# Strassen groups whose outer pairs alternate product by product, and the end of an attention head on VectorE alone

## The chip, the cores and the metric

The kernel runs on one core of one Trainium2 chip. The metric is the device time of one execution in microseconds (us); a kernel is timed several times and its median is taken. The engines are TensorE (PE, matrix products; PEld is its loading of weights), VectorE (DVE), ScalarE (ACT), GpSimd (POOL) and SyncE (SP), whose queue issues the transfers.

## What is computed

One step of a layer with two branches on the same normalised input, for 2048 frames of a new stream and 64 frames of a running one (2112 rows, 17 blocks of 128 of which the last, "the sample", has 64 rows). Everything is fp32.

```
xn = rms_norm(x, norm_gain);  u = xn @ w_in
xa, za, q, k, v, zb, ga, gb = split_in(u)
h, h_last = rglru(conv(xa), ...);      ya = h * silu(za)
q = rms_norm(q per head half);         k = rms_norm(k per head half)
o = diff_attn(q, k, v, ...)            # softmax minus lam * softmax
yb = rms_norm(o) * subln_gain * ... * silu(zb)
m = sigmoid(ga) * (ya @ w_proj_a) + sigmoid(gb) * (yb @ w_proj_b)
y = x + m @ w_out
```

## The kernel before

**Products.** An fp32 product is made of three matmuls on halves: each operand is cut into a high part (ScalarE's cast) and a low part (a subtraction), and high by high, high by low and low by high are added up in PSUM (lines 63, 64 and 65).

**Stages.** The Hawk branch (to about 492 us), stage a (six projections of 1024 columns: v, q/k of heads 0 to 3, zb, q/k of heads 4 to 7, ga, gb, to about 1625 us), the attention (eight heads, to about 2596 us), and stage d (out_a, out_b, out_y). Stages a and d are objects of the class `Stage`, which runs *groups*; a group is one 2112x1024 by 1024x1024 product.

**A Strassen group.** The 16 whole blocks of x form eight *pairs* (block i and block i+8). The weight is cut in four quarters, a pair into four too, and a Strassen-Winograd scheme makes seven products of 12 matmuls instead of eight for each pair, 56 products a group. Seven weights are needed: B11, B21, B22 and T1 to T4. The sample block takes five short slots without Strassen, at the end of the group. A *slot* is one product on TensorE; `tick()` closes it, `at(slot, task)` places the work of the other engines in a slot, and the four engines run in this written order (`manual_schedule`); only SP's queue is ordered by a scheduler.

**Around the products.** `plan_w` says in which slot a weight is loaded, subtracted (`sub`, line 126, VectorE, in two halves) and cut (`cut`: ScalarE line 133, then low halves on VectorE and GpSimd, line 135). `plan_x` does the same for the x of a pair: S1 and S2 on VectorE, S3 and S4 on GpSimd (line 163), high halves on ScalarE (167), low halves on VectorE (S2 and A12) and GpSimd (the other five) (170). `pair` issues the seven products and takes them out of PSUM: five additions on VectorE (217, 223, 228, 238, 243) and two copies on ScalarE (213, 233). What is done with the result depends on the group. In a q/k group the squares are summed (763), the inverse root is made (776, 780, 55 to 57), the two results are scaled (785) and, some slots later, transposed by TensorE (800) and taken out on ScalarE and VectorE (815, 817). In gates it is a sigmoid (735), for zb a product as well (740).

**The end of a head.** The head's result `o` lies in SBUF as 17 blocks. `finish` makes an inverse root `y` per row with Newton steps (1151 to 1155, 55 to 57). For heads 0 to 6 GpSimd multiplies each block by its column of y (1186); then `weigh` loads up to four blocks of the gate, `zt`, and GpSimd multiplies (1166). `part` transposes the block on TensorE (1173), VectorE scales the result into `yt` (1175) and SP stores it to yb_d (1176). For the last head VectorE does both products. `zt` and `yt` have two buffers each. Meanwhile the next head works: its maxima are taken by VectorE straight from PSUM (950, 1062), and its sums of exponentials are combined by GpSimd (975, 976).

## Time and profile before

| | us |
|---|---|
| median of three runs | 3159.47 (3156.75 to 3160.89) |
| the profiled execution's own time | 3151.77 |
| its span | 3150.0 |
| TensorE busy | 2858.8 |
| VectorE / ScalarE / GpSimd busy | 2107.5 / 1624.6 / 1647.2 |
| stage a / attention / stage d, about | 1132 / 970 / 546 |

Busy times of the engines overlap; they don't add up to the span. The span is the part of the execution that the trace covers, 1.8 us less than its time. TensorE's mean granted clock was 0.959 of full speed.

### The profile page before, as it was taken

To read this page: it belongs to the slowest core of one execution; us is meant where nothing else is said; L and a number is where in the kernel's file an instruction comes from. 1 tells how busy PE (TensorE), PEld (TensorE's weight loads), DVE (VectorE), ACT (ScalarE), POOL (GpSimd) and SP (SyncE) were. 2 spreads that over 40 slices of the span, in tenths; PEclk is the share of its full clock that TensorE was granted. 3 is DMA by queue.
4 is the path that set the end of the run, shared out by engine and by line. 5 is a ranking of instruction groups with operands and counts; after the bars stand their busy time and mean duration, and the time that the engine had idled before them with its cause. 6 is when DMAs were issued, how large, how long until landed. Compare 5 with 4: busy or idle time off the path is not lost. (4 is left out here: it accounts for less than half of the span.)

```text
span 3150.0 us, 44022 instructions
## 1 busy us (share of the span) xinstructions
PE 2858.8 (91%) x14808; PEld 2404.1 (76%) x14808; DVE 2107.5 (67%) x4074; ACT 1624.6 (52%) x3111; POOL 1647.2 (52%) x1145
## 2 busy tenths in 40 slices
PE   6999997999979899899989898898898879989898
PEld 6888885778768687687868787787787767868687
DVE  8777777378884888737346675675675774485864
ACT  7677764244453445534337666566576552233421
POOL 0000005475565755657535665565565557797853
PEclk9999998999989999999999999999999999999899
DMA  4121132345543446533366345344343334555453
GB/s 138 63 74 60 67 107 94 119 137 150 178 153 121 132 145 180 163 107 117 110 166 172 105 116 140 102 119 137 98 123 108 107 97 154 184 190 204 158 171 127
DMA packets 356674, 408.99 MB, mean 130 GB/s; under 512 B 48448, under 2 KB 242400, under 8 KB 356448
## 3 DMA queue, kind: packets, MB, share of 16 engines
q1 hardware_dynamic: 356448, 406.18, 41.9%
q8 instruction: 118, 1.93, 0.3%
q14 instruction: 108, 0.88, 0.1%
HBM read 272.22 MB, written 131.37 MB: 128 GB/s over the span
## 5 line engine op out<-in xcount | busy, mean ns | idle before, releaser
L63 PE MATMUL acc<-w,xq 128*128 128x512 f32 x2016 | 810.7, 402 | 31.0 <-DVE s L223 16.4
L64 PE MATMUL acc<-w,xq 128*128 128x512 f32 x2016 | 800.2, 397 | 31.4 <-DVE w L135 29.0
L65 PE MATMUL acc<-w,xq 128*128 128x512 f32 x2016 | 800.4, 397 | 9.6 <-POOL xq L170 9.5
L170 POOL TENSOR_TENSOR xq<-xq 128x512 fp32r<-128x512 f32 x360 | 535.5, 1500 | 377.7 <-ACT xq L167 236.3
L163 POOL TENSOR_TENSOR xq<-xq 128x512 f32<-128x512 f32 x144 | 203.1, 1410 | 551.7 <-DVE xq L163 547.7
L63 PEld LDWEIGHTS acc<-w,xq 128*128 128x128 f32 x2016 | 387.8, 192 | 120.3 <-issue 30.3
L64 PEld LDWEIGHTS acc<-w,xq 128*128 128x128 f32 x2016 | 387.8, 192 | 112.9 <-DVE w L135 31.5
L65 PEld LDWEIGHTS acc<-w,xq 128*128 128x128 f32 x2016 | 387.2, 192 | 95.4 <-POOL xq L170 10.6
L167 ACT CAST xq<-xq 128x512 fp32r<-128x512 f32 x504 | 297.6, 619 | 27.7 <-DVE xq L163 13.7
L1003 PE MATMUL accv<-v,tw 128*128 128x128 f32 x2176 | 302.6, 283 | 8.0 <-ACT o L1015 8.0
L950 DVE TENSOR_SCALAR_CACHE_REDUCE S<-pk,far 128x1024 f32<-128x1024 f32 x224 | 225.7, 1014 | 120.9 <-PE pk L938 112.9
L937 PE MATMUL pk<-k,Q 128*128 128x512 f32 (+2 forms) x640 | 270.8, 424 | 29.5 <-DVE mp L958 17.8
L1003 PEld LDWEIGHTS accv<-v,tw 128*128 128x128 f32 x2176 | 278.0, 198 | 12.7 <-ACT o L1015 10.1
L968 ACT ACTIVATE S<-S,nm 128x1920 f32<-128x1920 f32 (+7 forms) x128 | 208.9, 1632 | 70.3 <-DVE nm L967 68.9
L233 ACT COPY s<-acc 128x512 f32<-128x512 f32 x72 | 42.2, 587 | 391.7 <-PE acc L65 366.4
L996 ACT COPY tw<-ptt 128x512 f32<-128x512 f32 (+1 forms) x288 | 157.4, 556 | 160.2 <-PE ptt L995 158.8
L938 PE MATMUL pk<-k,Q 128*128 128x512 f32 (+2 forms) x640 | 236.6, 376 | 1.6 <-DMA Q<-ql_d 1.5
L64 PE MATMUL accb<-x,wh 128*128 128x384 f32 (+3 forms) x656 | 232.9, 355 | 2.9 <-DVE x L503 2.9
L63 PE MATMUL accb<-x,wh 128*128 128x384 f32 (+3 forms) x656 | 234.4, 357 | 0.2 <-ACT x L502 0.2
L976 POOL TENSOR_TENSOR S<-S,S 128x2048 f32<-128x2048 f32 (+3 forms) x64 | 230.3, 3599 | 4.2
L65 PE MATMUL accb<-x,wl 128*128 128x384 f32 (+3 forms) x656 | 232.4, 354 | 0.0
L975 POOL TENSOR_SCALAR S<-S,cf 128x2048 f32<-128x2048 f32 (+3 forms) x64 | 102.6, 1603 | 238.0 <-DVE cf L974 115.2
(244 smaller groups left out, 5561.8 us busy)
## 6 DMA issues: line engine op xcount, KB each, us to landing
xq<-xn_d SPq DMA_DIRECT2D x192, 256.0 KB, 3.9
w<-in_wg SPq DMA_DIRECT2D x72, 512.0 KB, 5.4
Q<-qh_d SPq DMA_DIRECT2D x128, 128.0 KB, 2.9
Q<-ql_d SPq DMA_DIRECT2D x128, 128.0 KB, 2.9
raw<-in_ckT SPq DMA_DIRECT2D x32, 512.0 KB, 3.7
raw<-in_cv SPq DMA_DIRECT2D x32, 512.0 KB, 3.9
raw<-in_w1b SPq DMA_DIRECT2D x32, 256.0 KB, 3.0
ya_d<-SZ SPq DMA_DIRECT2D x16, 512.0 KB, 3.3
```

The lines of the kernel that those rows point to most:

```text
L63: nc.tensor.matmul(out, shi, mhi, start=start, stop=False, **kw)
L64: nc.tensor.matmul(out, shi, mlo, start=False, stop=False, **kw)
L65: nc.tensor.matmul(out, slo, mhi, start=False, stop=stop, **kw)
L163: eng.tensor_tensor(q[dst], q[x], q[y], op=op)
L167: nc.scalar.copy(xs[nm][0], q[nm])
L170: eng.tensor_tensor(xs[nm][1], q[nm], xs[nm][0].bitcast(F32), op=ALU.subtract)
L937: nc.tensor.matmul(pk[:, o], Q[0][:, m, qs], kk, start=True, stop=False)
L938: nc.tensor.matmul(pk[:, o], Q[1][:, m, qs], kk, start=False, stop=True)
L950: nc.vector.tensor_scalar(s[:, k0 : k0 + f], pk[:, :f], far[:, h : h + 1], None, op0=ALU.add, op1=ALU.max, accum_out=mp[:, cx["j"] : cx["j ...
L968: nc.scalar.activation(s[:, :n], s[:, :n], AF.Exp, bias=nm, accum_out=sc[m])
L976: nc.gpsimd.tensor_tensor(S[0][:, :n], S[0][:, :n], S[1][:, :n], op=ALU.add)
L1003: nc.tensor.matmul(acc[:, r, :], tw[:, j, :], hd[kt // 8][1][:, kt % 8, :], start=kt == r == 0, stop=kt == 2 * p + 1)
```

## The change

Four things are changed.

1. **Order of the pairs.** The items of a group are now `(0, 1)`, `(2,)`, `(3,)`, the sample, `(4,)`, `(5,)`, `(6, 7)`. In `(0, 1)` and `(6, 7)` the two pairs alternate product by product, so a weight serves two products in a row and the next one is wanted two slots later. The order of the products is A11·B11, S1·T1, S2·T2, A12·B21, S3·T3, S4·B22, A22·T4.
2. **Sums in PSUM.** S2·T2, S3·T3 and A22·T4 are added onto the bank of A11·B11 (`bx`), S4·B22 onto that of S1·T1 (`by`). Of a pair VectorE makes three additions (lines 234, 238, 242 after the change) and ScalarE four copies.
3. **Plans.** The weights' subtractions and cuts stand in other slots: counted from the group's start, T1's subtraction -7, B11's cut -6, T2's subtraction -5, T1's cut -4, T2's cut -2, the subtractions of T3 and T4 both -1, the cuts of B21, T3, B22, T4 at 0, 2, 4, 6. VectorE makes three low halves of a pair's x (S2, A12, A22) and the sample's, GpSimd four. q and k are taken out of PSUM in the slot of their transposes. Buffers are rings for each kind.
4. **End of a head.** Scaling by y and product with zt are one VectorE instruction per block (scalar_tensor_tensor, line 1172 after the change) for every head; `zt` has three buffers. GpSimd does neither any more.

The core of the diff:

```
-ITEMS = [0, 1, 2, 3, 4, 5, 6, 7, "s"]
+ITEMS = [(0, 1), (2,), (3,), "s", (4,), (5,), (6, 7)]
...
-        at(b - 16, lambda: (load("B11", 0), load("B12", 1)))
-        at(b - 13, lambda: sub("T1", "B12", "B11"))
-        at(b - 10, lambda: load("B22", 3))
-        at(b - 9, lambda: (load("B21", 2), cut("B11")))
-        at(b - 7, lambda: sub("T2", "B22", "T1"))
-        at(b - 6, lambda: cut("T2"))
-        at(b - 5, lambda: sub("T3", "B22", "B12", "B12"))
-        at(b - 4, lambda: sub("T4", "B21", "T2", "T2"))
-        for i, nm in enumerate(("T3", "T1", "B21", "T4", "B22")):
-            at(b - 3 + i, lambda nm=nm: cut(nm))
+        at(b - 13, lambda: (load("B11", 0), load("B12", 1)))
+        at(b - 8, lambda: load("B22", 3))
+        at(b - 7, lambda: sub("T1", "B12", "B11"))
+        at(b - 6, lambda: cut("B11"))
+        at(b - 5, lambda: sub("T2", "B22", "T1"))
+        at(b - 4, lambda: (load("B21", 2), cut("T1")))
+        at(b - 2, lambda: cut("T2"))
+        at(b - 1, lambda: (sub("T3", "B22", "B12", "B12"), sub("T4", "B21", "T2", "T2")))
+        for i, nm in enumerate(("B21", "T3", "B22", "T4")):
+            at(b + 2 * i, lambda nm=nm: cut(nm))
...
+        off = b - s[0]
+        for nm, k, eng in zip(("A11", "S1", "S2", "A12", "S3", "S4", "A22"), s, (G, G, V, V, G, G, V)):
+            at(k + off - 4, lambda nm=nm: hi(nm))
+            at(k + off - 3, lambda nm=nm, eng=eng: lo(nm, eng))
...
+        bx, p1 = bank(), self.small()
+        prod(bx, "A11", "B11", True)
+        nc.scalar.copy(p1, bx)
+        yield
+        by, p5 = bank(), self.small()
+        prod(by, "S1", "T1", True)
+        nc.scalar.copy(p5, by)
+        yield
         u2 = self.small()
+        prod(bx, "S2", "T2", False)
+        nc.scalar.copy(u2, bx)
+        yield
+        bz = self.pz.tile([P, 512], F32, name="acz")
+        prod(bz, "A12", "B21", True)
+        V.tensor_tensor(p1, p1, bz, op=ALU.add)
+        done(item, 0, p1)
+        yield
+        prod(bx, "S3", "T3", False)
+        V.tensor_tensor(p5, p5, bx, op=ALU.add)
+        done(item + 8, 1, p5)
+        yield
+        prod(by, "S4", "B22", False)
+        V.tensor_tensor(u2, u2, by, op=ALU.add)
+        done(item, 1, u2)
+        yield
+        prod(bx, "A22", "T4", False)
         c21 = self.small()
+        nc.scalar.copy(c21, bx)
         done(item + 8, 0, c21)
...
-                zt = wk.tile([P, 4, P], F32, name="zt")
+                zt = wk.tile([P, 4, P], F32, name="zt", bufs=3)
...
-                eng = nc.gpsimd if h < NH - 1 else nc.vector
-                eng.tensor_tensor(o[:tn, b : b + nb, :], o[:tn, b : b + nb, :], zt[:tn, :nb, :], op=ALU.mult)
-                book("pool" if h < NH - 1 else "dve", pe[0] + 2.0, 0.33 * nb)
+                for j in range(nb):
+                    k = b + j
+                    nc.vector.scalar_tensor_tensor(
+                        o[:tn, k, :], o[:tn, k, :], y[:tn, k - t0 : k - t0 + 1], zt[:tn, j, :],
+                        op0=ALU.mult, op1=ALU.mult,
+                    )
+                book("dve", pe[0] + 2.0, 0.25 * nb)
...
-            for j in range(t0 if h < NH - 1 else whole, t0 + n):
-                tn = TOK[j][1]
-                nc.gpsimd.tensor_scalar(
-                    o[:tn, j, :], o[:tn, j, :], y[:tn, j - t0 : j - t0 + 1], 1.0, op0=ALU.mult, op1=ALU.mult
-                )
-                book("pool", pe[0] + 2.0, 0.35)
```

VectorE at the end of a head, before: the last Newton steps, then the next head's work (cf is a factor of the softmax, SA and SB hold scores, mps their maxima).

```order
L55 SCALAR_TENSOR_TENSOR e_17032<-yo 128x17
L56 TENSOR_TENSOR e_17032<-e_17032,q_15301 128x17
L57 SCALAR_TENSOR_TENSOR yo<-e_17032,yo 128x17
L973 RECIPROCAL cf<-s_16602 128x1
L1062 TENSOR_SCALAR SA,mps<-pk,far 128x1024
L974 SCALAR_TENSOR_TENSOR cf<-cf,s_16601,neglam 128x1
L1062 TENSOR_SCALAR SA,mps<-pk,far 128x1024
L1062 TENSOR_SCALAR SB,mps<-pk,far 128x1024
L1062 TENSOR_SCALAR SB,mps<-pk,far 128x896
L1067 ISA SB,mps<-pk,bands 128x128
L1067 ISA mps 128x1
L1175 TENSOR_SCALAR yt<-ptt,gs 128x512
```

The same place after the change:

```order
L55 SCALAR_TENSOR_TENSOR e_16566<-yo 128x17
L56 TENSOR_TENSOR e_16566<-e_16566,q_14876 128x17
L57 SCALAR_TENSOR_TENSOR yo<-e_16566,yo 128x17
L1172 SCALAR_TENSOR_TENSOR o<-o,yo,zt 128x128 x12
L978 RECIPROCAL cf<-s_16183 128x1
L1067 TENSOR_SCALAR SA,mps<-pk,far 128x1024
L1172 SCALAR_TENSOR_TENSOR o<-o,yo,zt 128x128 x4
L979 SCALAR_TENSOR_TENSOR cf<-cf,s_16182,neglam 128x1
L1172 SCALAR_TENSOR_TENSOR o<-o,yo,zt 64x128
L1067 TENSOR_SCALAR SA,mps<-pk,far 128x1024
L1184 TENSOR_SCALAR yt<-ptt,gs 128x512
L1067 TENSOR_SCALAR SB,mps<-pk,far 128x1024
```

The 17 new instructions stand directly behind the Newton steps, 12 of them ahead of the first maximum of line 1067 (1062 before).

VectorE where the first q/k group passes into zb, before (217 to 243 are additions from PSUM, 763 a sum of squares, 817 an eviction of q, 126 and 135 a weight's subtraction and low half):

```order
L763 TENSOR_REDUCE va<-s_7925 128x8
L817 SCALAR_TENSOR_TENSOR s_8019<-ptx,gq,s_8017 128x512
L243 TENSOR_TENSOR s_7833<-s_7833,acc 128x512
L135 TENSOR_TENSOR w_8047<-w_8001,w_8046 128x1024
L763 TENSOR_REDUCE va<-s_7962 128x8
L776 TENSOR_SCALAR va<-va 128x16
L817 SCALAR_TENSOR_TENSOR s_8067<-ptx,gq,s_8065 128x512
L126 TENSOR_TENSOR w_7693<-w_7898,w_7693 128x1024 x2
L780 RECIPROCAL ya<-sra 128x16
L55 SCALAR_TENSOR_TENSOR tmpa<-ya 128x16
L56 TENSOR_TENSOR tmpa<-tmpa,va 128x16
L57 SCALAR_TENSOR_TENSOR ya<-tmpa,ya 128x16
```

The same passage after the change (775 is the sum of squares, 787, 792 and 55 to 57 the inverse root, 797 the scales, 828 the eviction of q, 135 a weight's subtraction, 145 its low half, 181 the low half of an x):

```order
L797 TENSOR_TENSOR sc<-sc,ya 128x512 x2
L775 TENSOR_REDUCE va<-sf 128x8
L135 TENSOR_TENSOR w_7617<-w_7763,w_7617 128x1024 x2
L135 TENSOR_TENSOR w_7856<-w_7882,w_7856 128x1024 x2
L775 TENSOR_REDUCE va<-sf 128x8
L145 TENSOR_TENSOR w_8008<-w_7882,w_8007 128x1024
L828 SCALAR_TENSOR_TENSOR sf<-ptx,gq,sf 128x512
L775 TENSOR_REDUCE va<-sf 128x8
L787 TENSOR_SCALAR va<-va 128x16
L181 TENSOR_TENSOR x_8013<-xS_7859,x_8013 128x512
L828 SCALAR_TENSOR_TENSOR sf<-ptx,gq,sf 128x512
L792 RECIPROCAL ya<-ya 128x16
```

The subtractions of T3 and T4 stand together now, and the roots and scales of two pairs one behind the other around them; the next root and its scales follow behind these rows.

SP's queue where gb, the last group of stage a, passes into the attention, before (gb_d takes the group's results, 64x512 are the sample's; Q, k and bands are loads of the attention):

```order
L737 DMA gb_d<-s_14150 128x512
L737 DMA gb_d<-s_14058 128x512
L882 DMA k_14307<-kl_d 64x2x1024
L911 DMA Q_14301<-qh_d 64x2x256
L912 DMA Q_14301<-qh_d 64x2x256
L911 DMA Q_14304<-ql_d 64x2x256
L261 DMA s_14213<-s_14211 64x512
L912 DMA Q_14304<-ql_d 64x2x256
L261 DMA s_14225<-s_14223 64x512
L898 DMA band<-strip_d 64x256
L899 DMA band<-strip_d 64x192
L900 DMA band<-neg 64x64
L737 DMA gb_d<-s_14211 64x512
```

The same place after the change:

```order
L749 DMA gb_d<-sc 128x512
L1108 DMA vn<-out_v 64x128
L1046 DMA raw<-in_ckT 128x1024 x3
L749 DMA gb_d<-sc 128x512
L886 DMA k_14259<-kh_d 64x2x1024
L749 DMA gb_d<-sc 128x512 x2
L887 DMA k_14259<-kl_d 64x2x1024
L916 DMA Q_13876<-qh_d 64x2x256
L917 DMA Q_13876<-qh_d 64x2x256
L916 DMA Q_13879<-ql_d 64x2x256
L917 DMA Q_13879<-ql_d 64x2x256
```

The loads of Q stood ahead of the sample's stores to gb_d; now all stores to gb_d stand ahead of them.

## Rows read from the trace of the kernel before

**Rows 1.** The page's busy time and share of the span of each engine.
```profile
PE 2858.8 (91%) x14808; PEld 2404.1 (76%) x14808; DVE 2107.5 (67%) x4074; ACT 1624.6 (52%) x3111; POOL 1647.2 (52%) x1145
```

**Rows 2.** What TensorE waited for, whole span: us in total, times, longest.
```profile
PE ptt L1173 <- DVE yt L1175: 31.5, 5, 7.6
PE ptx L800 <- DVE s L785: 30.7, 14, 7.3
PE acc L64 <- DVE w L135: 29.0, 6, 7.9
PE ptt L1173 <- POOL o L1166: 28.7, 17, 4.2
```

**Rows 3.** Stretches of the v and first q/k group: length, busy us of engines, clock.
```profile
492.30:682.90 190.60, 177.47 (x730) 138.92 (x730) 97.81 (x96) 64.71 (x106) 103.00 (x67) 0.94 0.37 118
682.90:892.50 209.60, 186.18 (x831) 148.44 (x830) 184.94 (x243) 97.11 (x178) 124.77 (x81) 0.95 0.50 152
```

**Rows 4.** A stretch behind a head's last wait, same columns: PEclk is the granted clock.
```profile
1905.90:1912.70 6.80, 4.41 (x17) 4.13 (x18) 4.71 (x25) 2.37 (x6) 0.00 (x0) 0.50 0.45 123
```

**Rows 5.** Timeline of GpSimd at one head's end: start, length, instruction.
```profile
1882.37 5.91 POOL L1186 TENSOR_SCALAR o<-o,yo 128x128 f32<-128x128 f32 x17
...
1889.50 1.65 POOL L975 TENSOR_SCALAR S<-S,cf 128x1664 f32<-128x1664 f32 x1
...
1892.34 3.72 POOL L976 TENSOR_TENSOR S<-S,S 128x1664 f32<-128x1664 f32 x1
1896.03 2.50 POOL L1166 TENSOR_TENSOR o<-o,zt 128x512 f32<-128x512 f32 x2
```

**Rows 6.** Timeline of SP's queue in the same stretch.
```profile
1892.41 5.36 SPq L1162 DMA_DIRECT2D zt<-zb_d  x2
```

**Rows 7.** Timeline of VectorE in the same stretch; brackets hold its idle time.
```profile
1907.39 0.75 DVE L1175 TENSOR_SCALAR yt<-ptt,gs 128x512 f32<-128x512 f32 x1 [13.51 <-DMA yb_d<-yt]
```

**Rows 8.** Line 437 on VectorE: duration in ns, min/median/max, first and last start.
```profile
L437 DVE SCALAR_TENSOR_TENSOR wl<-raw,chan,wh x128: 342/347/360, 9.3 to 425.5; 128x128 fp32r<-128x128 f32 x128
```

**Rows 9.** Chain that ended last, from 3141 us: start, length, what.
```profile
3141.02 0.23 PE acc L254
...
3142.37 2.25 DMA s<-s
```

**Rows 10.** VectorE by line in stage a: busy us and mean ns of one.
```profile
L170 DVE TENSOR_TENSOR xq<-xq 128x512 fp32r<-128x512 f32 x96 | 96.4, 1004 | 0.0
L135 DVE TENSOR_TENSOR w<-w,w 128x1024 fp32r<-128x1024 f32 x40 | 86.2, 2174 | 4.1 <-ACT w L133 4.1
L126 DVE TENSOR_TENSOR w<-w,w 128x1024 f32<-128x1024 f32 x40 | 68.3, 1750 | 0.0
L785 DVE TENSOR_TENSOR s<-s,ya 128x512 f32<-128x512 f32 (+1 forms) x68 | 56.8, 877 | 1.2
L763 DVE TENSOR_REDUCE va<-s 128x8 f32<-128x512 f32 (+1 forms) x68 | 46.0, 677 | 0.0
...
L55 DVE SCALAR_TENSOR_TENSOR tmpa<-ya 128x16 f32<-128x16 f32 (+1 forms) x34 | 22.6, 664 | 1.2
```

**Rows 11.** TensorE's waits from 855 to 905 us, first q/k group to zb.
```profile
PE ptx L800 <- DVE s L785: 14.7, 3, 7.3
```

**Rows 12.** TensorE's waits from 490 to 530 us, start of stage a.
```profile
PE acc L65 <- POOL xq L170: 6.7, 1, 6.7
PE acc L64 <- DVE w L135: 6.2, 1, 6.2
```

**Rows 13.** TensorE's waits from 2590 to 2615 us, start of stage d.
```profile
PE acc L63 <- ACT w L133: 5.5, 1, 5.5
```

**Rows 14.** DMA issues on the page: transfers, KB each, median us to landing.
```profile
Q<-qh_d SPq DMA_DIRECT2D x128, 128.0 KB, 2.9
```

**Rows 15.** VectorE at 863.37 on the timeline, and a table of the stretch around it.
```profile
863.37 4.49 DVE L785 TENSOR_TENSOR s<-s,ya 128x512 f32<-128x512 f32 x2
...
861.50:868.30 6.80, 3.40 (x16) 2.33 (x15) 6.66 (x8) 3.21 (x5) 5.42 (x3) 1.00 0.55 171
```

More of the change, by code (lines that the diff above doesn't have):

```diff
@@ L122, in sub @@
         def sub(dst, x, y, over=None):
[L123 removed]
+            q[dst] = q[over] if over else self.wtile(pick=pick)
             for i in range(2):
@@ L232, in pair, with prod @@
-        c11 = self.small()
-        nc.scalar.copy(c11, b1)
-        done(item, 0, c11)
-        self.tick()
-        self.product(b3, x["A22"], w["T4"], False, True, True)
+        def prod(out, a, b, first):
+            self.product(out, x[a], w[b], first, True, not first)
+            if item == 7:
+                self.wfree.extend(w[b][2])
+        bx, p1 = bank(), self.small()
[3 more added lines that the diff above has]
+        by, p5 = bank(), self.small()
@@ L289, in run @@
             ws = {}
-            self.plan_w(wsrc, ws, b)
-            for it in ITEMS:
-                xs = {}
-                self.plan_x(xsrc, it, xs, b - 5 if it == 0 and b > 0 else b)
-                plan.append((it, xs, ws, out, b))
-                b += 5 if it == "s" else 7
+            last = g == len(groups) - 1 and self.first
+            self.plan_w(wsrc, ws, b, False if last else None)
+            for its in ITEMS:
+                n = len(its)
+                gens = []
+                for k, it in enumerate(its):
+                    xs = {}
+                    s = [b + i for i in range(5)] if it == "s" else [b + n * i + k for i in range(7)]
+                    self.plan_x(xsrc, it, xs, s, s[0] - 1 if it == 4 else s[0])
+                    gens.append((it, xs, ws, out, s))
+                plan.append((gens, b))
+                b += 5 if its == "s" else 7 * n
         self.now = -20
@@ L300, in run @@
         self.c.enter_context(self.tc.manual_schedule(engines={E.PE, E.DVE, E.Activation, E.Pool}))
-        for it, xs, ws, out, b in plan:
+        for items, b in plan:
             assert self.now == b
-            done = out(it, b)
-            if it == "s":
-                self.sample(xs, ws, done)
-            else:
-                self.pair(it, xs, ws, done)
+            gens = []
+            for it, xs, ws, out, s in items:
+                done = out(it, s)
+                if it == "s":
+                    self.sample(xs, ws, done)
+                else:
+                    gens.append(self.pair(it, xs, ws, done))
+            for _ in range(7 if gens else 0):
+                for g in gens:
+                    next(g)
+                    self.tick()
         while self.tasks:
```

231 lines of the change are left out of this document (95 added, 136 removed).

## The prediction

> **What bounds the kernel now.** I first read the page's share of each engine [rows 1]: TensorE is busy for 2858.8 us of the 3150.0 us span, so an edit to the other engines can win at most the 291 us in which TensorE is idle, and some of the time in which it works at the lower of its two clock levels. Next comes the table of what TensorE waits for [rows 2]. It names two families. The first is the end of an attention head: the transposes of line 1173 wait 31.5 us for VectorE's copy of line 1175 and 28.7 us for GpSimd's product of line 1166, 60.2 us together. The second is the passage from one Strassen group to the next: 30.7 us for line 785 (the scale of q and k before they are transposed) and 29.0 us for line 135 (the low half of a weight). Third, the table of stretches [rows 3]: the v group needs VectorE for 97.81 us of 190.60, the first q/k group for 184.94 us of 209.60. So VectorE has room in a plain group and hardly any in a q/k group. Last, the granted clock: after the last wait of a head, 1905.9 to 1912.7 us shows 0.50 [rows 4], 1.2 of 2.4 GHz. In these 6.8 us half of the speed is lost, 3.4 us of work, so a wait costs more than its own length.
>
> **The end of a head.** GpSimd first scales the 17 blocks of a head (5.91 us), then multiplies them in groups by the gate z, 1.25 us a group, and between these stands its own work for the next head, 1.65 and 3.72 us [rows 5]. So the third and fourth products end only at 1898.5, 16 us after the scalings began at 1882.37. SP's queue is held up by that: z has two buffers, the third and fourth loads of z occupy SP for 5.36 us from 1892.41 [rows 6], and the stores of yt stand behind them. VectorE's third copy then sits idle for 13.51 us until a store has freed yt's buffer [rows 7], and TensorE with it. The change makes scaling and product one VectorE instruction per block, and gives z a third buffer.
>
> The trace has no such instruction in the attention. The nearest row is line 437, the same operation at 128x128: 128 times, median 347 ns [rows 8]. I take 0.35 us: 17 are 5.9 us a head, and 12 of them, 4.2 us, stand at once behind the Newton steps. The first three groups of o are then ready after about 4.2 us, z's loads no longer wait for GpSimd, and yt's stores leave early. The bounds: all of the 60.2 us goes, with 3.4 us of clock in each of the seven heads that use GpSimd, 24 us, together -84; or nothing is won, since the 4.2 us stand ahead of the next maxima (line 1062, after the change 1067) and TensorE waits there instead. I expect something between: 3 us a head stay for yt's store, as yt still has two buffers, 21 us, which leaves 39; half of the clock's 24 comes back, 12; and the 4.2 us ahead of the maxima cost TensorE 1.5 us a head, 10 us, because several PSUM buffers cover the rest. The sum is **-41 us**.
>
> **The groups.** TensorE's work does not change: the same products of 12 matmuls at 0.23 us [rows 9], 2.76 us a product. Sixteen PSUM additions a group leave VectorE for ScalarE's copies and for sums in PSUM, but eight low halves a group come to it from GpSimd, so its load falls little. What counts is which of its instructions stand in the slots at a passage. I go through the one from q/k to zb, with the new order and the mean durations of this stage [rows 10]. Between the last addition (line 242) and the scale that the first late transposes need there stand: three inverse roots with their two scales, each three steps of 0.66 and two of 0.88, 3.75 us, 11.2 in all; two cuts of 2.17, 4.3; the four halves of T3's and T4's subtractions of 1.75, 7.0; four sums of squares of 0.68, 2.7; one low half, 1.0; and two evictions of q, which I take at 0.7 like the sums, 1.4. That is 27.6 us. TensorE has six products for it, 16.6 us, and waits 11. The next transposes need a scale that stands behind another 7.6 us (a sum of squares, a cut, a low half, a root with two scales), against one product: 4.8 us more. Together that is 16 us, less a us or two that the transposes themselves take. The same wait before, for line 785, is 14.7 us [rows 11]. So the alternation gives each weight twice the time, but it also brings the evictions of two pairs into the same slots, and this passage stays as long as it is.
>
> I take **+5 us** for all seven passages together, a little more than nothing for the low halves that VectorE now makes. Bounds: -40, if the waits for line 135 go (29.0) and a clock stretch at three passages with them (10); and +73, if at each of the seven passages TensorE waits for T3's and T4's subtractions in full (7.0) and loses 3.4 us of clock.
>
> **Ends of the stages.** The first group of stage a waits 6.7 us for the low half of an x and 6.2 us for line 135 [rows 12]. With pairs 0 and 1 alternating, each weight is wanted only 5.5 us after the one before it: **-9 us** (0 to -13). The first group of stage d waits 5.5 us for its first weight [rows 13]; the second one is wanted after two products, no longer after one: **-4 us** (0 to -7, or +5 if the new steps of the last head hold the weight up). At the end of the program the sample's half sum goes through a DMA of 2.25 us [rows 9]; with the sample in the middle of the group 28 products hide it: **-3 us** (0 to -4). At the passage to the attention SP's queue has the last stores of gb_d ahead of the first loads of Q, which stood ahead of the sample's stores; these stores leave only after the last product, and a load of Q takes 2.9 us to land [rows 14], and three more are issued with it: **+5 us** (0 to 8).
>
> The sum is -41 + 5 - 9 - 4 - 3 + 5 = -47 us. The profiled execution took 3151.8 us (span 3150.0 and 1.8 around it), so 3105 for one like it. The median shown, 3159.5, lies 7.7 us higher; less 47 it gives 3112. I say **3110 us**.
>
> **A rule that speaks against it.** Two scales of line 785 took 4.49 us from 863.37, in a stretch where GpSimd worked for 5.42 of 6.80 us [rows 15], against 0.88 each in the mean. So VectorE loses time beside GpSimd. The Trainium skill, page "SBUF — State Buffer", section "Who interferes with whom", says that a VectorE instruction with two SBUF inputs contends with a GpSimd instruction that reads SBUF, and that the later one blocks for a whole instruction; the 4.49 us agree in sign. By that rule the sum above would lose what rival A takes.
>
> **Rivals.**
> *A: the head's new steps get stuck behind GpSimd.* Freed of its 5.91 us, GpSimd starts its 1.65 and 3.72 us at once, just when the 12 steps stand. If both hold VectorE for their whole length, the maxima come 9.6 us late instead of 4.2; 5.4 us a head more reach TensorE, 38 us in seven heads, and the 12 us of clock do not come back: 3110 + 50 = 3160, no change. For it: the 4.49 us. Against it: line 437 kept to 347 ns, though with an idle GpSimd.
> *B, slower: the passages.* The evictions of two pairs, the low halves moved to VectorE and the subtractions of T3 and T4 (all four at one slot) fall together at each passage, and the upper bound of 73 comes true in place of 5: 3178. For it: 184.94 of 209.60. Against it: in plain groups VectorE is half idle. It decides from 55 us over what I took, 8 us at each passage.
> *C: the weights come in time everywhere*, -40 in place of +5: 3065. For it: 29.0 us of waits for line 135. Against it: the sum at q/k to zb.
> *D: the head's waits only change their names*, since the store that frees yt, with its two buffers, still comes last (31.5 of the 60.2). Only the 28.7 us for line 1166 go, and 10 of them are lost at the maxima: -19 in place of -41, 3132.
>
> **Chances.** The forecast 0.42, C 0.14, D 0.15, A 0.11, B 0.18. A measurement of this kernel can't tell a change of less than about 0.2%, 6 us, from none. Faster: the forecast, C, D and a little of A and B, 0.70; same: most of A, 0.09; slower: the rest of B and A, 0.21. The range goes from 3055 to 3175: it takes in C, D and A and leaves out the worse half of B and the end of C.
>
> **What would show it.** In the changed profile the waits at line 1173 (its number will shift) should fall from 60 to about 21 us, the new operation should take 0.35 to 0.45 us, and TensorE's waits for the maxima (lines 937 and 1058) should rise by no more than 10 us or so. The waits at the ends of the q/k groups should still be for the scale, some 15 us each, and the entry to stage a nearly without one. The prediction is wrong if the new operation's mean is near 0.6 us (A), or if the waits at the passages double (B) or vanish (C).

## The result

The changed kernel takes 3129.49 us (median of three runs, 3126.71 to 3132.76) against 3159.47: a ratio of 0.9907, with a 95% interval from 0.9884 to 0.9929. Its profiled execution has a span of 3131.0 us, 19.0 less than before; the timed runs of before lie higher than its profiled one, so the medians are 30 us apart. The stretches below go by the spans.

First the stretches of the changed kernel from the table of stretches (length; busy us of PE, PEld, DVE, ACT, POOL with instructions; granted clock; DMA share; GB/s): stage a, attention, stage d, each from its first to its last product, then the first q/k group, which answers to [rows 3], and zb, the group behind it.

```profile
490.10:1649.60 1159.50, 1054.64 (x4562) 846.30 (x4560) 686.99 (x873) 551.02 (x951) 568.94 (x363) 0.95 0.43 136
1649.60:2553.80 904.20, 823.79 (x5623) 717.86 (x5622) 655.46 (x2105) 596.79 (x1260) 485.22 (x294) 0.97 0.46 126
2553.80:3126.70 572.90, 526.15 (x2283) 422.59 (x2283) 350.44 (x343) 207.62 (x353) 376.31 (x230) 0.95 0.51 167
686.10:884.20 198.10, 184.75 (x817) 148.98 (x816) 147.22 (x215) 100.67 (x182) 107.85 (x68) 0.94 0.51 154
884.20:1083.80 199.60, 174.79 (x745) 141.18 (x744) 130.25 (x153) 96.55 (x165) 96.82 (x60) 0.93 0.40 131
```

The three stretches, and zb, of the kernel before:

```profile
492.30:1624.80 1132.50, 1049.17 (x4561) 842.10 (x4560) 752.13 (x904) 493.11 (x857) 659.12 (x426) 0.96 0.44 137
1624.80:2590.30 965.50, 839.73 (x5632) 736.23 (x5633) 637.35 (x2013) 605.99 (x1268) 566.97 (x451) 0.95 0.44 122
2590.30:3141.70 551.40, 520.84 (x2274) 421.13 (x2272) 337.80 (x324) 174.56 (x295) 408.00 (x258) 0.96 0.51 170
892.60:1066.20 173.60, 166.63 (x731) 135.57 (x730) 115.31 (x135) 81.74 (x138) 109.54 (x68) 0.98 0.43 140
```

Stage a has become 27.0 us longer (1132.5 to 1159.5), the attention 61.3 shorter (965.5 to 904.2) and stage d 21.5 longer (551.4 to 572.9); the start is 2.2 us earlier, and what follows the last product is 4.0 shorter (8.3 to 4.3). That makes the 19.0. So a large gain and a large loss stand behind a small difference.

Within the stages the loss has its places. Counted from a group's first product to the next group's, to about 0.2 us, v takes 5.5 us more than before, the two q/k groups take 11.7 and 13.3 less, zb and ga behind them 26.0 and 24.6 more, gb 4.1 less; in stage d out_a takes 14.4 more, out_b 3.7 less, out_y 10.8 more. A q/k group and the one behind it together lose 14.3 and 11.3 us: 25.6 of the 27.0 of stage a.

What TensorE waits for in the changed kernel, over the whole span (answers to [rows 2]):

```profile
PE acc L65 <- POOL x L181: 55.4, 13, 18.1
PE acc L65 <- DVE x L181: 27.3, 11, 4.5
PE ptx L812 <- DVE sf L828: 23.7, 5, 8.7
...
PE pk L1063 <- DVE SA L1067: 17.1, 4, 4.3
...
PE acc L64 <- DVE w L145: 10.8, 2, 6.1
...
PE pk L942 <- DMA Q<-ql_d: 9.7, 1, 9.7
...
PE ptt L1182 <- DVE o L1172: 1.9, 2, 1.1
```

The 60.2 us of waits at the ends of heads 0 to 6 are gone (the 1.9 of line 1182, 1173 before, is the last head's, where VectorE's products had cost 7.2); in their place TensorE waits 17.1 us in four heads for the maxima of line 1067. In the groups the weights' waits (29.0 to 10.8) and the scale's (30.7 to 2.5) have fallen, and waits for low halves of x (line 181) on GpSimd and VectorE and for the eviction of q (828) have come, which add up to more.

The end of a head on VectorE's timeline (answers to [rows 5] to [rows 7]):

```profile
1802.92 6.66 DVE L1172 SCALAR_TENSOR_TENSOR o<-o,yo,zt 128x128 f32<-128x128 f32 x12
1809.51 1.27 DVE L1067 TENSOR_SCALAR_CACHE_REDUCE SA<-pk,far 128x1024 f32<-128x1024 f32 x1
...
1811.91 1.39 DVE L1172 SCALAR_TENSOR_TENSOR o<-o,yo,zt 128x128 f32<-128x128 f32 x5
...
1816.30 0.75 DVE L1184 TENSOR_SCALAR yt<-ptt,gs 128x512 f32<-128x512 f32 x1 [1.20 <-PE ptt L1182]
...
1820.53 0.74 DVE L1184 TENSOR_SCALAR yt<-ptt,gs 128x512 f32<-128x512 f32 x1
```

and on GpSimd's and SP's, from the same time:

```profile
1802.83 3.72 POOL L981 TENSOR_TENSOR S<-S,S 128x1664 f32<-128x1664 f32 x1
```

```profile
1813.07 0.91 SPq L1167 DMA_DIRECT2D zt<-zb_d  x2
...
1817.87 0.98 SPq L1185 DMA_DIRECT2D yb_d<-yt  x2
```

What SP waited for at z's loads, in the kernel before from 1880 to 1912 us (us in total, times, longest):

```profile
SPq L1162 <- POOL o L1166: 16.5, 3, 10.1
```

and in the changed kernel from 1800 to 1826 us:

```profile
SPq L1167 <- DVE o L1172: 11.1, 4, 7.3
```

All blocks of o are ready at 1813.3, some ten microseconds after the Newton steps; before, the sixteen whole ones alone took 16. SP still stands at z's loads, now for VectorE, but earlier: the last of them has left at 1814.0, ahead of the first copy into yt (1816.30), where before it left at 1900.2, ten microseconds behind the first copy (1890.26). So the first stores of yt leave right behind the first copies, and the third copy (1820.53) waits for nothing. But the first twelve instructions took 6.66 us, where the last five took 1.39, 0.28 each: they started at 1802.92, 0.09 us behind a GpSimd instruction of 3.72 us.

Line 1172 in two views, the durations (ns, min/median/max) and the group with its mean:

```profile
L1172 DVE SCALAR_TENSOR_TENSOR o<-o,yo,zt x136: 335/343/3773, 1802.9 to 2572.0; 128x128 f32<-128x128 f32 x128, 64x128 f32<-64x128 f32 x8
```

```profile
L1172 DVE SCALAR_TENSOR_TENSOR o<-o,yo,zt 128x128 f32<-128x128 f32 (+1 forms) x136 | 52.9, 457 | 3.0 <-DMA zt<-zb_d 2.7
```

The median is 343 ns; the mean of 457 comes from the few instructions that were held. The longest is the first of the head above, on the timeline by itself:

```profile
1802.92 3.77 DVE L1172 SCALAR_TENSOR_TENSOR o<-o,yo,zt 128x128 f32<-128x128 f32 x1
```

So it is in three of the four heads in which TensorE waits for line 1067. In the fourth the hold falls on a Newton step ahead of the new instructions, which then keep their pace, 0.27 us each:

```profile
2456.00 3.58 DVE L57 SCALAR_TENSOR_TENSOR yo<-e,yo 128x17 f32<-128x17 f32 x1
...
2460.26 3.24 DVE L1172 SCALAR_TENSOR_TENSOR o<-o,yo,zt 128x128 f32<-128x128 f32 x12
```

In all four GpSimd's instruction before that one, of 1.67 us, holds a Newton step too, for 1.5 us where an unheld one takes 0.18. In the other three heads neither of the two stands beside these steps, the twelve take 3.24 us, and TensorE doesn't wait for the maxima.

The first group of stage a, from 490 to 530 us, in TensorE's waits (answers to [rows 12]):

```profile
PE acc L65 <- POOL x L181: 18.1, 1, 18.1
```

### The profile page after: what moved, and what is told of

It reads as the page before. It is cut to its first block, busy times and chain, and to the rows that moved or that the text cites. A ratio compares the mean times of both kernels' runs of the same rounds, so it can differ in the third digit from the quotient of the medians.

```text
span 3131.0 us, 43652 instructions
## 1 busy us (share of the span) xinstructions
PE 2854.5 (91%) x14808; PEld 2392.7 (76%) x14808; DVE 2070.2 (66%) x4147; ACT 1703.7 (54%) x3251; POOL 1447.7 (46%) x900
## 4 chain that ended last, share of the span: by engine, by line
PE 45%; DVE 11%; ACT 4%; issue 2%; POOL 2%; DMA 1%; SPq 0%; DVEq 0%; POOLq 0%; ACTq 0%
PE acc L65 7%; PE acc L63 7%; PE acc L64 7%; PE accv L1008 5%; PE pk L942 3%; PE pk L943 3%; PE ptt L1000 3%; PE accv L1131 2%; PE acz L65 1%; PE acz L63 1%; PE acz L64 1%; DVE o L1172 1%; DVE S L955 1%; ACT S L973 1%; DVE w L135 1%
## 5 line engine op out<-in xcount | busy, mean ns | idle before, releaser
L65 PE MATMUL acc<-w,x 128*128 128x512 f32 x1728 | 694.9, 402 | 82.8 <-POOL x L181 55.4
L63 PE MATMUL acc<-w,x 128*128 128x512 f32 x1728 | 699.0, 405 | 14.8 <-ACT sc L230 7.7
L64 PE MATMUL acc<-w,x 128*128 128x512 f32 x1728 | 689.0, 399 | 11.2 <-DVE w L145 10.8
L65 PEld LDWEIGHTS acc<-w,x 128*128 128x128 f32 x1728 | 334.8, 194 | 168.6 <-POOL x L181 64.1
L145 POOL TENSOR_TENSOR w<-w,w 128x1024 fp32r<-128x1024 f32 x63 | 180.1, 2860 | 574.7 <-ACT w L143 549.4
L63 PEld LDWEIGHTS acc<-w,x 128*128 128x128 f32 x1728 | 335.7, 194 | 87.1 <-ACT sc L230 8.5
L64 PEld LDWEIGHTS acc<-w,x 128*128 128x128 f32 x1728 | 335.2, 194 | 81.8 <-DVE w L145 11.8
L181 POOL TENSOR_TENSOR x<-xA,x 128x512 fp32r<-128x512 f32 x144 | 217.3, 1509 | 311.9 <-ACT x L178 298.2
L942 PE MATMUL pk<-k,Q 128*128 128x512 f32 (+2 forms) x640 | 263.2, 413 | 48.8 <-DVE S L955 17.7
L1008 PE MATMUL accv<-v,tw 128*128 128x128 f32 x2176 | 295.7, 279 | 2.6 <-ACT o L1020 2.3
L181 POOL TENSOR_TENSOR x<-xS,x 128x512 fp32r<-128x512 f32 x144 | 209.9, 1462 | 54.0 <-ACT x L178 52.1
L943 PE MATMUL pk<-k,Q 128*128 128x512 f32 (+2 forms) x640 | 231.6, 368 | 0.0
L181 DVE TENSOR_TENSOR x<-xA,x 128x512 fp32r<-128x512 f32 x144 | 145.8, 1012 | 122.9 <-ACT x L178 122.9
L178 ACT CAST x<-xA 128x512 fp32r<-128x512 f32 x288 | 177.3, 621 | 75.0 <-PE acc L65 38.2
```

Of the source, the lines that this page charges most:

```text
L63: nc.tensor.matmul(out, shi, mhi, start=start, stop=False, **kw)
L64: nc.tensor.matmul(out, shi, mlo, start=False, stop=False, **kw)
L65: nc.tensor.matmul(out, slo, mhi, start=False, stop=stop, **kw)
L145: eng.tensor_tensor(lo[:, s, :], raw[:, s, :], hi.bitcast(F32)[:, s, :], op=ALU.subtract)
L178: nc.scalar.copy(xs[nm][0], q[nm])
L181: eng.tensor_tensor(xs[nm][1], q[nm], xs[nm][0].bitcast(F32), op=ALU.subtract)
```

## The experiments

Each was timed beside the kernel before, on the same chip; ratios are to the kernel before. The changed kernel's is 0.9907 [0.9884, 0.9929], from the timing above.

| run | ratio | 95% interval |
|---|---|---|
| head's end alone | 0.9801 | 0.9787 to 0.9816 |
| groups alone | 1.0127 | 1.0110 to 1.0143 |
| other places for the first weights | 0.9915 | 0.9900 to 0.9930 |
| T4's subtraction later | 0.9911 | 0.9897 to 0.9926 |
| cuts a slot earlier | 0.9970 | 0.9958 to 0.9982 |
| q's low half on GpSimd | 0.9892 | 0.9878 to 0.9907 |
| gb_d's stores on ScalarE's queue | 0.9938 | 0.9919 to 0.9957 |
| these five together | 0.9932 | 0.9910 to 0.9953 |
| low halves back on GpSimd | 0.9967 | 0.9956 to 0.9978 |
| root and scale later | 0.9877 | 0.9863 to 0.9892 |
| three banks for transposes | 0.9952 | 0.9933 to 0.9970 |
| head's end and q on GpSimd | 0.9792 | 0.9777 to 0.9807 |

**The head's end alone.** The kernel before, with only this:

```
-                zt = wk.tile([P, 4, P], F32, name="zt")
+                zt = wk.tile([P, 4, P], F32, name="zt", bufs=3)
...
-                eng = nc.gpsimd if h < NH - 1 else nc.vector
-                eng.tensor_tensor(o[:tn, b : b + nb, :], o[:tn, b : b + nb, :], zt[:tn, :nb, :], op=ALU.mult)
-                book("pool" if h < NH - 1 else "dve", pe[0] + 2.0, 0.33 * nb)
+                for j in range(nb):
+                    k = b + j
+                    nc.vector.scalar_tensor_tensor(
+                        o[:tn, k, :], o[:tn, k, :], y[:tn, k - t0 : k - t0 + 1], zt[:tn, j, :],
+                        op0=ALU.mult, op1=ALU.mult,
+                    )
+                book("dve", pe[0] + 2.0, 0.25 * nb)
...
-            for j in range(t0 if h < NH - 1 else whole, t0 + n):
-                tn = TOK[j][1]
-                nc.gpsimd.tensor_scalar(
-                    o[:tn, j, :], o[:tn, j, :], y[:tn, j - t0 : j - t0 + 1], 1.0, op0=ALU.mult, op1=ALU.mult
-                )
```

> The kernel before with only the end of a head changed (one VectorE step per block, three buffers of z); groups as before. Theory: the change is a gain in the attention and a loss in the groups. A head's period fell from 119.4 us to 101 and 117 in turn, mean 109, so seven heads give 70 us: about 3090 us against 3159, and faster than the full change (3129). Rival: the groups are neutral as I forecast, and only the two starts (stage a, first loads of Q) lost about 15 us in the full change: then about 3115. If the steps on VectorE only gain together with the new groups, about 3150.

Measured: 3092.01 us against 3153.29, 61 less. Its stretches, stage a, attention and stage d:

```profile
494.60:1628.50 1133.90, 1048.92 (x4561) 842.08 (x4560) 752.57 (x904) 492.91 (x856) 658.39 (x426) 0.96 0.44 137
1628.50:2530.50 902.00, 824.74 (x5634) 717.45 (x5633) 660.82 (x2140) 601.12 (x1268) 488.61 (x296) 0.97 0.47 131
2530.50:3082.80 552.30, 519.13 (x2274) 420.06 (x2273) 335.87 (x324) 174.55 (x295) 408.23 (x258) 0.96 0.51 170
```

The two stages are those of before to within 1.5 us (1132.5 and 551.4), and the attention is 63.5 us shorter. The theory holds, the rival (3115) doesn't.

**The groups alone.** The changed kernel with `weigh` and `finish` of before, the first experiment's diff turned round.

> The changed kernel with the old end of a head (GpSimd scales and multiplies, two buffers of z). Theory: the groups alone lose some 40 us, so 3195 to 3200 us, slower than before (3159). Rival, groups neutral but for the starts: 3165 to 3175. If the groups gain: under 3155.

Measured: 3192.98 us against 3153.29, 40 more. Its stretches:

```profile
488.40:1647.60 1159.20, 1053.12 (x4562) 844.99 (x4560) 687.08 (x873) 550.80 (x952) 568.62 (x363) 0.95 0.43 136
1647.60:2607.00 959.40, 841.30 (x5622) 738.28 (x5622) 623.99 (x1986) 600.92 (x1259) 562.55 (x447) 0.94 0.42 118
2607.00:3186.10 579.10, 524.19 (x2283) 422.37 (x2283) 350.74 (x335) 208.14 (x353) 374.95 (x231) 0.95 0.51 166
```

Stage a is 26.7 us longer than before and stage d 27.7, the attention 6.1 shorter, since d's first products stand among the last head's transposes. To within the noise the two halves add up: 0.9801 x 1.0127 is 0.9925, inside the interval of the whole change.

**Other places for the first weights.** In the changed kernel's trace the low half of T2 is held by the stores of ya_d, whose source lies in the same place; GpSimd is idle for 12.09 us until 509.75. The edit:

```
-        S = Stage(nc, tc, c, "a", ident, [2, 3, 0, 4, 5, 1, 6, 9, 8, 10, 11, 14, 12, 13, 7], dict(c=9, f=8), (0, 1, 2))
+        S = Stage(nc, tc, c, "a", ident, [2, 3, 0, 4, 5, 1, 6, 9, 8, 10, 11, 7, 12, 13, 14], dict(c=9, f=8), (0, 1, 2))
...
+        at(-3, lambda: S.wfree.sort(key=lambda p: p > 11))
```

> The changed kernel with other places in SBUF for the first group's weights in stage a, so that the low halves of T2 and B21 don't wait for the stores of ya_d, which read the buffer that lay there. Theory: in the change GpSimd stood until 509.7 us for these stores, the low half of S1 was queued behind T2's and B21's cuts, and TensorE waited 18.1 us with some 10 us more at half clock; now the wait falls to under 5 us and the time to about 3110. Rival: the low half of S1 is late anyway, since ScalarE's casts come behind the Hawk branch's last functions; wait still over 10 us, time 3125 to 3130.

Measured: 0.9915, no difference from the changed kernel's 0.9907. The wait at this place fell by half, in TensorE's waits from 490 to 530 us:

```profile
PE acc L65 <- POOL x L181: 9.4, 1, 9.4
```

and stage a became 3.9 us shorter in the profile. GpSimd now makes its halves of T2's and B21's cuts from 500.96 us on, but the low half of S1 stands behind them all the same:

```profile
500.96 6.10 POOL L145 TENSOR_TENSOR w<-w,w 128x1024 fp32r<-128x1024 f32 x2 [3.00 <-ACT w L143]
507.02 2.24 POOL L181 TENSOR_TENSOR x<-xS,x 128x512 fp32r<-128x512 f32 x1
```

So the place was one cause of the 18.1 us, and GpSimd's queue the next; the theory's 18 us in time did not come.

**T4's subtraction later.**

```
-        at(b - 1, lambda: (sub("T3", "B22", "B12", "B12"), sub("T4", "B21", "T2", "T2")))
+        at(b - 1, lambda: sub("T3", "B22", "B12", "B12"))
+        at(b + 1, lambda: sub("T4", "B21", "T2", "T2"))
```

> The changed kernel with the subtraction of T4 two slots later (slot +1 in place of -1). Theory: the waits at the passages are for low halves of x that stand on VectorE behind the two subtractions; 3.5 us less at each of seven passages, with some clock, 15 to 25 us: about 3110. Rival: GpSimd's queue or ScalarE's casts are what is late, and nothing moves: 3125 to 3133; or T4's cut is late now and it is slower.

Measured: 0.9911, no difference. The waits for VectorE's eviction of q fell from 23.7 to 19.1 us, those for GpSimd's low halves rose from 55.4 to 63.4. The theory falls.

**Cuts a slot earlier.**

```
-        at(b - 6, lambda: cut("B11"))
+        at(b - 7, lambda: cut("B11"))
...
-        at(b - 4, lambda: (load("B21", 2), cut("T1")))
-        at(b - 2, lambda: cut("T2"))
+        at(b - 5, lambda: (load("B21", 2), cut("T1")))
+        at(b - 3, lambda: cut("T2"))
...
-            at(b + 2 * i, lambda nm=nm: cut(nm))
+            at(b + 2 * i - 1, lambda nm=nm: cut(nm))
```

> The changed kernel with each weight's cut one slot earlier. Theory: at q/k to zb ScalarE's cast of a weight stands behind its new copy of a product, which TensorE has first to make; GpSimd's half of the cut waits for that cast, and the low halves of x wait behind it, so that TensorE waits 7.1 us for line 181 on GpSimd. One slot earlier the cast stands ahead of that copy: the waits for GpSimd's line 181 fall from 55 us to about 30 and the time by 15 to 25 us, to about 0.985 of before. Rival: GpSimd is late for other reasons or the wait moves to VectorE's low halves; 0.989 to 0.993 as now.

Measured: 0.9970, about 20 us slower than the changed kernel. TensorE's waits:

```profile
PE acc L65 <- DVE x L181: 38.1, 15, 8.2
PE acc L65 <- POOL x L181: 33.8, 21, 3.7
PE ptx L812 <- DVE sf L828: 28.9, 6, 11.1
PE acc L64 <- DVE w L145: 26.5, 3, 10.9
```

GpSimd's low halves came as much earlier as expected (55.4 to 33.8), but VectorE's low halves (27.3 to 38.1), q's eviction (23.7 to 28.9) and the weights' halves (10.8 to 26.5) came later by more. The link from ScalarE's copy to GpSimd was there; taking it away only changes who is late.

**q's low half on GpSimd.**

```
-                nc.scalar.mul(hi.bitcast(F32R), pq, gq)
-                lo = new()
-                nc.vector.scalar_tensor_tensor(lo.bitcast(F32R), pq, gq, hi, op0=ALU.mult, op1=ALU.subtract)
+                qf, lo = new(), new()
+                nc.scalar.mul(qf, pq, gq)
+                nc.scalar.copy(hi.bitcast(F32R), qf)
+                nc.gpsimd.tensor_tensor(lo.bitcast(F32R), qf, hi, op=ALU.subtract)
```

> The changed kernel with q taken out of PSUM as k is: ScalarE copies, GpSimd makes the low half from SBUF, VectorE does nothing. Theory: the transposes' two PSUM banks (three before) come free only when VectorE, behind its weights, has read them; TensorE's waits of line 812 for line 828, 23.7 us, vanish, with the half clock behind them: 20 to 30 us, about 0.983. Rival: the freed waits come back at the next thing that is late, the low halves of x, and the gain is under 10 us.

Measured: 0.9892, within the interval of the changed kernel. The 23.7 us became 17.2 for ScalarE's copy from the same bank, and GpSimd's low halves 62.2. The rival holds; the trace's stage a is 8.8 us shorter.

**The stores of gb_d on ScalarE's queue.**

```
-                            nc.sync.dma_start(to, sg[:tn])
+                            q = nc.scalar if dst is gb_d and item in (6, 7) else nc.sync
+                            q.dma_start(to, sg[:tn])
```

> The changed kernel with the gb_d stores of the last two pairs issued by ScalarE's queue in place of SP's. Theory: the first loads of Q stand behind these stores on SP; TensorE's wait for Q, 9.7 us, falls to about 1 and the half clock of 10.2 us behind it with it: 10 to 14 us, about 0.987. Rival: the wait is for Q's loads themselves or for k's, which stand ahead: nothing changes.

Measured: 0.9938, no gain. TensorE still waited 8.9 us for Q. SP's queue had no such store left, and its waits from 1640 to 1656 us show what held the last of Q's first loads (line 918):

```profile
SPq L918 <- DMA gb_d<-sc: 3.9, 1, 3.9
```

Here Q's load waits for the store from `sc` to land, though another queue issues it. The likely reason is that Q's buffer lies where `sc` lay in stage a, as a place is handed on; no run shows it. In the changed kernel SP has no such wait: its 6.6 us there are for ScalarE's sigmoids, whose results the stores take ahead of Q. So the order in the queue, my step, was one link, and taking it away left a second one, with 8.9 us of waiting in place of 9.7.

**These five together** (other places, T4 later, cuts earlier, q on GpSimd, gb_d by ScalarE; their diffs as above).

> All of these together in the changed kernel: cuts a slot earlier, T4's subtraction two slots later, q by GpSimd, the places of the first weights, gb_d's stores on ScalarE's queue. Theory: each removes its own wait and the groups cost no more than before; 40 to 60 us under the changed kernel, 0.972 to 0.978, which would beat the kernel with the head's end alone (0.980). Rival: the mended waits come back elsewhere, since VectorE is the bound of the q/k groups: 0.980 to 0.987.

Measured: 0.9932. The waits for VectorE's low halves rose to 58.6 us, those for q's eviction by VectorE are gone. The rival's direction holds, and it is worse than it said: none of these five shifts, alone or together, brought the groups back.

**The low halves back on GpSimd.**

```
-                    V.tensor_tensor(o[:, i, :, TS:], r, o.bitcast(F32)[:, i, :, :TS], op=ALU.subtract)
+                    G.tensor_tensor(o[:, i, :, TS:], r, o.bitcast(F32)[:, i, :, :TS], op=ALU.subtract)
...
-        for nm, k, eng in zip(("A11", "S1", "S2", "A12", "S3", "S4", "A22"), s, (G, G, V, V, G, G, V)):
+        for nm, k, eng in zip(("A11", "S1", "S2", "A12", "S3", "S4", "A22"), s, (G, G, V, V, G, G, G)):
```

> The changed kernel with the low halves of A22 and of the sample made by GpSimd, as before the change. Theory: VectorE is what ends last at the passages, and these nine instructions of about 1 us a group are part of its load there: the wait falls by some 2 us at each of seven passages, 15 us, ratio to before about 0.986. Rival: the low halves were not late on VectorE for their own length; GpSimd's low halves, already waited for with 55 us, come later still: 0.991 to 0.998.

Measured: 0.9967, some 19 us slower than the changed kernel. The waits for GpSimd's low halves rose from 55.4 to 73.4, those for VectorE's fell from 27.3 to 9.1. The rival holds: moving these low halves to VectorE is a part of the change that pays.

**Root and scale later.**

```
-                    at(S.now + 2, root)
-                    at(S.now + 3, scale)
+                    at(S.now + 3, root)
+                    at(S.now + 4, scale)
```

> The changed kernel with the inverse root and the scale of q and k one slot later (sums of squares and transposes stay). Theory: in the middle of a q/k group, behind the sample, ScalarE's square root waits for VectorE's sum, ScalarE's copy of a product stands behind it, and TensorE waits 3.8 us for that copy (line 230) with half clock behind; one slot of slack removes it: the waits for line 230, 7.7 us, go to 0, some 10 to 15 us in all, ratio about 0.987. Rival: the scale is now late for the transposes, and TensorE's wait of line 812 for line 797 takes its place: 0.990 to 0.995.

Measured: 0.9877; the interval (to 0.9892) just overlaps that of the changed kernel (from 0.9884), and stage a is 15.6 us shorter in the profile (1143.9). The wait for line 230 is gone, that for the scale came up from 2.5 to 23.0:

```profile
PE ptx L812 <- DVE sc L797: 23.0, 8, 7.5
```

Both were right in part; of the shifts in the groups it is the one that comes nearest to helping, but no gain over the changed kernel is clear of the noise.

**Three banks for the transposes, one for A12 B21.**

```
-        self.pz = pool("pz", 2, space=PSUM)
-        self.pt = pool("pt", 2, space=PSUM)
+        self.pz = pool("pz", 1, space=PSUM)
+        self.pt = pool("pt", 3, space=PSUM)
```

> The changed kernel with three PSUM banks for transposes, as before the change, and one in place of two for the product A12 B21. Theory: with two banks the third transposes wait until VectorE has read the first; with three the 23.7 us of line 812 for line 828 fall to under 10 with their half clock, and a single bank for A12 B21 costs little, since VectorE adds it at once: 15 to 20 us, ratio about 0.985. Rival: at the outer pairs two such products stand in a row, and the second waits for VectorE's addition: 0.990 to 1.0.

Measured: 0.9952. The 23.7 us became 16.7, but 13.1 us of waits for the single bank (line 63 for VectorE's line 234) came, 13 times, and VectorE's low halves rose to 34.0. The rival holds.

**The head's end, and q on GpSimd, in the kernel before.** The first experiment's diff, and the q path as k's:

```
-                    nc.scalar.mul(hi.bitcast(F32R), pq, gq)
-                    lo = new()
-                    nc.vector.scalar_tensor_tensor(lo.bitcast(F32R), pq, gq, hi, op0=ALU.mult, op1=ALU.subtract)
-                    put(ql_d, lo)
+                    qf = new()
+                    nc.scalar.mul(qf, pq, gq)
+                    nc.scalar.copy(hi.bitcast(F32R), qf)
+                    at(S.now + 1, lambda: rest(qf, hi))
...
-                put(kl_d, lo)
+                put(kl_d if isk else ql_d, lo)
```

> The kernel with only the end of a head changed (first experiment, 0.980), and q taken out of PSUM by ScalarE with the low half on GpSimd. Theory: VectorE bounds the q/k groups, 184.94 of 209.60 us; 17 evictions of 0.73 us a group, 25 us over two groups, leave it; the waits for line 785 fall by 10 to 15 us: 0.976. Rival: GpSimd's additional work slows VectorE's instructions beside it, or what is late is only what stands at the passage: 0.979 to 0.982.

Measured: 0.9792, not to be told from the 0.9801 without it. The waits for line 785 are 35.2 us (30.2 without it), so the scale did not come forward. Nor did VectorE get any freer. Stage a of this run (to be read beside the first line of the first experiment):

```profile
492.20:1624.20 1132.00, 1045.93 (x4561) 840.36 (x4560) 770.57 (x870) 513.77 (x890) 712.70 (x460) 0.96 0.44 137
```

VectorE has 34 instructions fewer, 24.9 us, and yet is busy for 18.0 us more (752.57 to 770.57), while GpSimd is busy for 54.3 more: its other instructions take longer, a root's step of line 55 0.83 us in place of 0.67 in the mean. The rival holds, in its first reason: GpSimd's additional work cost VectorE more time than the evictions had.

## Why the prediction was right

**The direction was right, and half of the reason.** I forecast a gain of 41 us at the ends of the heads, the groups and the ends of the stages about even (-6 us), and 3110 us; it is 3129, inside the range. The heads gained 61 and the rest lost 40. The two errors, 20 us too little gain and 46 too little loss, have opposite signs, so that the sum came near is in part luck.

**The head's end: -41 forecast, -61 measured** (3092 against 3153, and 63.5 us of the attention in the profile). 15.0 of the 63.5 are TensorE's busy time (839.73 to 824.74 us, the granted clock 0.95 to 0.97), where I took 12 for the clock; the other 48.5 are waits, where my terms made 29. The instruction's price was right: 0.35 us taken from line 437 [rows 8], 0.343 in the median. Mis-sized was the residue. I kept 21 us for yt's store, because yt still has two buffers; in the changed kernel TensorE has no wait for it in any head. The store had been late because SP stood at z's loads, 16.5 us for GpSimd's products; with these earlier, the first stores leave at 1817.87, and two buffers do. My sum took this cause away and still kept what it causes. (The 5.36 us of [rows 6] I misread as the hold: they are two issues, of 0.37 and 0.47 us, the fourth load of z and the sample's, with a wait between.) The 10 us for the maxima were mis-sized the other way (17.1, in four heads of 4.3 each, in place of 1.5 in each): twelve steps, 3.24 us when nothing holds them, stand ahead of the first maximum, and two holds by GpSimd come on top, of 1.5 us at a Newton step and of 3.6 to 3.8 us at the first of the twelve or at another Newton step. So rival A's mechanism came, both instructions for their whole length, but in every second head only, and at 17.1 us in all.

**The rule of the page "SBUF — State Buffer"** (the Trainium skill, section "Who interferes with whom"), by which the later of two such instructions blocks for the whole of the other, agrees with this trace at the head's end: an instruction of 343 ns took 3.77 us when it began 0.09 us behind one of GpSimd's of 3.72 us, and in no head did it take longer.

**The passages: +5 forecast.** At q/k to zb I added up 16 us less the transposes' time; the waits there are, from 870 to 935 us of the changed kernel:

```profile
PE ptx L812 <- DVE sf L828: 8.4, 1, 8.4
PE acc L65 <- POOL x L181: 7.1, 1, 7.1
PE acc L65 <- DVE x L181: 4.2, 2, 2.7
PE acz L65 <- DVE x L181: 2.5, 1, 2.5
```

With two small ones it is 23.3 us, against 17.1 before (14.7 of them in [rows 11]); behind the second q/k group it is 25.0 against 15.7. That is more, but not the double that rival B wanted. The scale that I took as what ends last is hardly waited for any more (0.9); what is late is what stands beside it on the same queues, the eviction of q and the low halves of x. For the longest wait, 8.4 us, VectorE's row has T3's and T4's four subtractions ahead of the eviction:

```profile
902.52 4.61 DVE L135 TENSOR_TENSOR w<-w,w 128x1024 f32<-128x1024 f32 x4
...
908.79 0.74 DVE L828 SCALAR_TENSOR_TENSOR sf<-ptx,gq,sf 128x512 fp32r<-128x512 f32 x1
```

The adding up gave the size of the wait roughly, not its name, and 6 us too little here and 9 at the second group. It went by means, too. In the same passage a root with its two scales takes 9.4 us beside a busy GpSimd and the next one 2.2 beside an idle one:

```profile
892.60:902.00 9.40, 4.96 (x14) 3.72 (x14) 9.26 (x8) 5.84 (x10) 8.82 (x5) 0.58 0.19 58
914.60:916.80 2.20, 2.20 (x14) 1.81 (x13) 2.06 (x8) 0.00 (x0) 0.10 (x1) 1.00 0.89 262
```

What I held against the new steps of a head alone, in rival A, is at work here as well, before the change [rows 15] and after it.

**The starts: -9 and -4 forecast, both the wrong sign.** Stage a waits 18.1 us for the low half of S1 in place of 12.9; stage d 10.8 for weights' low halves and 7.1 for casts, in place of 5.5 [rows 13], 2.9 and 1.5. I counted the grace that alternation gives and not which buffers the new places lie on, nor that GpSimd's in-order queue has the low half of S1 behind two cuts.

**A stretch that I left out: the middle of the q/k groups.** The sample stands there now, five short slots, less time for the work that is planned into them. From 738 to 850 us TensorE waits 3.8 us for a copy by ScalarE that stands behind a square root, and 3.2 for the third pair of transposes' bank, and the granted clock is 0.50 behind each, from 746.9 to 753.7 and from 828.8 to 835.6; before, from 730 to 850 us, it waited nine times for 0.6 us at most and the clock stayed up:

```profile
738.00:850.00 112.00, 104.97 (x476) 84.54 (x475) 76.47 (x144) 59.05 (x114) 51.88 (x38) 0.94 0.60 178
870.00:935.00 65.00, 41.76 (x163) 32.35 (x162) 57.36 (x65) 29.27 (x50) 34.99 (x19) 0.79 0.20 63
1654.80:1665.00 10.20, 5.66 (x12) 3.70 (x13) 2.66 (x6) 0.00 (x0) 0.00 (x0) 0.50 0.82 197
```

```profile
730.00:850.00 120.00, 115.90 (x545) 93.99 (x544) 101.43 (x153) 57.98 (x112) 64.64 (x48) 1.00 0.56 168
```

In the sum over stage a the changed kernel's waits of TensorE for the groups' lines are about 105 us, before 83 (from the tables of waits of the two); 22 of the 27 us that the stage lost are these, the rest is TensorE's busy time, 1049.17 to 1054.64 us, at a granted clock of 0.96 before and 0.95 after. So the groups cost 40 us (second experiment) where my terms made -6: +5 for the passages, +5 for Q, -9, -4 and -3. The upper bound of 73 took it in.

**The passage to the attention: +5, measured 9.7 us of waiting** for Q, where a load takes 2.9 to land [rows 14], and from the middle of that wait on 10.2 us at a granted clock of 0.50, 1.2 GHz (last row of the changed kernel's stretches above). The size was too small, and the queue's order was not the only link, as the seventh experiment shows. The end of the program came out at the edge of what I said (-3, 0 to -4): the chain behind the last product is a copy of 0.59 us and an addition of 0.69 and the store, 4.0 us shorter.

**VectorE's load: "falls little".** From the kernel before to the changed one VectorE's busy time in stage a fell from 752.13 to 686.99 us and GpSimd's from 659.12 to 568.94, in the first q/k group VectorE's from 184.94 to 147.22. Yet TensorE waits more. So it isn't the sum of VectorE's work that costs the groups; over the short stretch from 870 to 935 us it is busy for 57.36 of 65.00 us.

What remains open: which part of the group plan costs the 40 us. The places are known (the q/k groups with the group behind them, the starts of both stages, and out_y), and the experiments find no mend in single shifts (T4's slot, the cuts' slot, the place of q's low half, the banks) and show that the low halves on VectorE are worth their move. Not tried was the old order of pairs with the new sums in PSUM, since it wants more places for weights than there are; the sample's place was not tried by itself either. That the order of the work on VectorE and GpSimd and their holding each other up set these waits, so that a shift only renames them, fits all eight runs on the groups but is argued, not shown. In the head's end no run separates the third buffer of z from VectorE's steps.

The best version is the head's end alone on the old groups, 0.980 of before, with or without q on GpSimd.

## What to carry to other kernels

Split a change into its independent halves before looking for the reason of a small difference: here -61 and +40 us, timed one by one, stood behind a change of -30, and the better kernel was one half. When an in-order queue is held (SP at z's loads), everything behind it is late, and a wait that looks like a want of buffers may vanish with the cause ahead of it. And in a passage where TensorE waits for several in-order queues in turn, count the short slots and each queue there, not only the wait that ended last before: in the eight runs on the groups the mended wait gave way to the next. And work moved from VectorE to GpSimd isn't simply off VectorE, as the last experiment shows.

## What was not expected of the hardware

An instruction of VectorE of 0.343 us took 3.773 us when it began just behind GpSimd's 128x1664 addition of 3.72 us, and the eleven behind it took 2.9 us together (6.66 less 3.77): the whole of one neighbour's instruction, once, not a slowing in proportion. And 24.9 us of work moved from VectorE to GpSimd left VectorE busy for 18.0 us more (last experiment).
